# Scans in place of the large reciprocals in the HGRN heads of an encoder block, with ScalarE's side steps pinned behind the weight casts

## The chip, the cores and the metric

The kernel runs on one core of one Trainium2 chip. Its time is device microseconds from start to end, median of 3 runs. TensorE multiplies matrices into PSUM; VectorE (DVE), ScalarE (ACT) and GpSimd (POOL) work on SBUF tiles of 128 partitions; SyncE (SP) issues most transfers. The engines run side by side, each working through its own instructions in a fixed order, and wait for one another by semaphores.

## The reference, cut to what matters

One encoder layer on x of 1024 tokens by 1024 features, all in float32:

```python
h = layer_norm(x, ln_in_g, ln_in_b)
proj = h @ w_in                                # 1024 x 11776
a = dilated_attention(aq, ak, av, slopes)      # 24 heads of 64, three dilations
r = hgrn2(hq, hf_fwd, hf_bwd, hi, hg, ...)     # 8 heads, 128 keys, 128 values
m = sigmoid(ga) * (a @ w_att_up) + sigmoid(gh) * (r @ w_hgrn_up)
h = layer_norm(alpha * h + m @ w_o, ...)
h = layer_norm(alpha * h + (silu(gate) * up) @ w_ffn_out, ...)
```

The change lies in `hgrn2`, in both directions of each head. With the forget gate f = lb + (1 - lb) * sigmoid(f_pre), the recurrence is computed in chunks of the time axis:

```python
cum = jnp.cumsum(log f, axis=time in chunk)
q_dec = q * exp(cum)             # the product of the gates up to a token
k_inv = k * exp(-cum)            # and its reciprocal, k = 1 - f
a = tril(q_dec @ k_inv^T);  o_intra = a @ v
u = (k * exp(cum_last - cum))^T @ v;  S' = exp(cum_last) * S + u
o = o_intra + q_dec @ S
```

So each token needs a running product of gates and the reciprocal of that product.

## The kernel before, in words

**Phase 1** is the input projection as a stream of weights. Its 92 tiles of 128 output columns are done four at a time; each group of four is 14 products (seven products of Strassen's scheme, for two pairs of tiles), and each product is 12 matmuls of 128 x 512, three for each of four blocks of 128 rows, because a float32 weight is split into a high and a low half. For a product, ScalarE casts the high half `w_hi` (L585, function `cast`), VectorE subtracts to get the low half `w_lo` (L590), and TensorE multiplies. `prep(i + 3)` does this three products ahead; four pairs of buffers take turns, so a cast waits until an earlier product has read its pair. Results are evacuated from PSUM by ScalarE (L606) and VectorE (L475, L486, L507).

**Side work.** The loop in `phase1` takes one product per turn and, after it, one part of a side unit. Units are the eight HGRN heads (`hgrn_side`) and, for each of four groups of attention heads, a far and a near part (`att_far`, `att_near`), in the order head, head, far, near. Each unit is a generator: a `yield n` lets n products go by before its next part, and a negative number also allows the next unit's inputs to be fetched. A unit begins when the stream has produced its inputs and the unit before has ended.

**A head's gate stage** is `hgrn_dir`, run for direction 0 and then 1, three parts each, one product apart. Time is laid out in 8 chunks of 128, each of two halves of 64: the "far" half and the "near" half. Part one: ScalarE turns the stored tanh into gates, tile A (the far half, L1262 and L1267) and tile B (the near half and one neighbour, L1263 and L1268), each with a column of zeros that restarts the product; GpSimd turns the tanh tile t in place into 1 - f (L1269); VectorE runs two scans (`tensor_tensor_scan`, L1274) that make running products of A and B in place, with restart constants `self.d1`; GpSimd multiplies the keys' near half by B (L1282). Part two: VectorE takes reciprocals of A, in two instructions of 128 x 256 (L1285), and GpSimd multiplies the keys' far half by them (L1286). Part three: two reciprocals of B (L1289), then the queries are multiplied by A and by the reciprocals (L1290, L1291), and GpSimd copies the chunk ends (L1295, L1296, L1298).

After the gate stage come the transposes of values and keys on TensorE (L905, L1306), copied by ScalarE (L906, L1307), the states (L1322, L1325, L1328, L1336), the scores (L1349 to L1353), the outputs (L1375) and a last transpose (L1411). Slots (`slot(n)`) are ten fixed tiles that the units share; `half` tiles are a ring of five.

**What sets the order.** The program is traced in the order of the Python code, and a planner with its own estimate of durations then puts each engine's instructions in order, by priority and by when it expects their inputs. Casts and evacuations are traced with `high_priority`. The opening and most of the feed-forward part are held in traced order by hand (`in_order`, which adds an order-only edge between neighbours on an engine). The stream and the side work of phase 1 are not: there the planner may put a side instruction ahead of the products that were traced before it.

**Phases 2 and 3** (the merge of attention and HGRN, the output projection, the feed-forward part) follow after about 1207 us and aren't touched.

Of the kernel before, what the change touches and what calls it, by code (L numbers as in the profile page):

```python
# [13 lines left out]
AF = mybir.ActivationFunctionType  # L14
OP = mybir.AluOpType
# [21 lines left out]
CQ = 0.5 * 128 ** -0.5  # L37
# [112 lines left out]
class Block:  # L150
# [405 lines left out]
    def stream(self, tiles):  # L556
# [5 lines left out]
        A = [{}, {}]  # L562
# [31 lines left out]
        def prep(i):  # L594
            if i >= len(seq):
                return
            with tc.high_priority(offset=self.evac_ahead):
                cast(i)
                rest(i, nc.vector)
# [25 lines left out]
        def evacuate(i, *later):  # L625
# [4 lines left out]
            with tc.high_priority(offset=self.evac_ahead):  # L630
# [10 lines left out]
                else:  # L641
                    pair[1](0, ps, None)

        first = 2 * len(self.ORDER)
        with self.pool("p0") as pool:
            self.lasts = {}
# [5 lines left out]
        for i, (n, g, p) in enumerate(seq):  # L652
            if i < first:
                continue
            sums(i + 5)
            prep(i + 3)
            if i < first + 2:
                continue
            product(i)
            evacuate(i)  # L660
            yield 4 * n + 2 * g + 2 if p == 4 else 0
# [588 lines left out]
    def hgrn_dir(self, h, d, st):  # L1250

        nc = self.nc
        ga, gb, gna = (z[:, d, h:h + 1] for z in (self.ga, self.gb, self.gna))
        t3 = st[f"t{d}"].rearrange("p (c i) -> p c i", i=128)
        q3 = st["q"].rearrange("p (c i) -> p c i", i=128)

        A = st["fa"][:, HALF * d:HALF * d + HALF].rearrange("p (c i) -> p c i", i=64)
        B = self.slot(7 + d, "fb", (8, 66))
        if d == 0:
            nc.gpsimd.memset(A[:, :, 0:1], 0.0)  # L1260
            nc.gpsimd.memset(B[:, :, 65:66], 0.0)
            nc.scalar.activation(A[:, :, 1:64], t3[:, :, 65:128], AF.Identity, bias=gb, scale=ga)  # L1262
            nc.scalar.activation(B[:, :, 0:65], t3[:, :, 0:65], AF.Identity, bias=gb, scale=ga)  # L1263
        else:
            nc.gpsimd.memset(A[:, :, 63:64], 0.0)
            nc.gpsimd.memset(B[:, :, 0:1], 0.0)
            nc.scalar.activation(A[:, :, 0:63], t3[:, :, 0:63], AF.Identity, bias=gb, scale=ga)  # L1267
            nc.scalar.activation(B[:, :, 1:66], t3[:, :, 63:128], AF.Identity, bias=gb, scale=ga)  # L1268
        nc.gpsimd.tensor_scalar(t3, t3, gna, ga, op0=OP.mult, op1=OP.add)  # L1269

        def scan(f, n, rev):
            f = f.rearrange("p c i -> p (c i)")
            f = f[:, ::-1] if rev else f
            nc.vector.tensor_tensor_scan(f, f, self.d1[n], 0.0, op0=OP.mult, op1=OP.add)  # L1274

        scan(A, 64, d == 1)
        scan(B, 66, d == 0)
        far = slice(64, 128) if d == 0 else slice(0, 64)
        near = slice(0, 64) if d == 0 else slice(64, 128)
        R = B[:, :, 1:65]  # L1280
        qd = self.slot(2 + 2 * d, "qd", (8, 128))
        nc.gpsimd.tensor_mul(t3[:, :, near], t3[:, :, near], R)  # L1282
        yield
        for c in (slice(0, 4), slice(4, 8)):
            nc.vector.reciprocal(qd[:, c, far], A[:, c])  # L1285
        nc.gpsimd.tensor_mul(t3[:, :, far], t3[:, :, far], qd[:, :, far])  # L1286
        yield
        for c in (slice(0, 4), slice(4, 8)):
            nc.vector.reciprocal(qd[:, c, near], R[:, c])  # L1289
        nc.vector.scalar_tensor_tensor(qd[:, :, far], q3[:, :, far], CQ, A, op0=OP.mult, op1=OP.mult)  # L1290
        nc.vector.scalar_tensor_tensor(qd[:, :, near], q3[:, :, near], CQ, qd[:, :, near], op0=OP.mult, op1=OP.mult)  # L1291
        st["qd", d], st["ki", d] = qd, t3

        dec = st["dec", d] = self.smt.tile([128, 2, 8], F32, name="dec", tag="dec", bufs=4)
        nc.gpsimd.tensor_copy(dec[:, 0, :], A[:, :, 63 if d == 0 else 0])  # L1295
        nc.gpsimd.tensor_copy(dec[:, 1, :], B[:, :, 0 if d == 0 else 65])  # L1296
        both = st["both", d] = self.smt.tile([128, 8], F32, name="both", tag="both", bufs=4)
        nc.gpsimd.tensor_mul(both, dec[:, 0, :], dec[:, 1, :])  # L1298
# [129 lines left out]
    def phase1(self):  # L1428
# [14 lines left out]
        work = self.stream(tiles)  # L1443
        there = next(work)
        self.slp = side.enter_context(self.pool("slp"))
        wait, pre, now, late, free = 0, None, None, -4, True
        for k in work:
            there = k or there
            if now:
                wait -= 1  # L1450
                if wait <= 0:
                    w = next(now, None)
                    if w is None:
                        now = None
                    free = free or w is None or w < 0
                    wait = abs(w or 0)
            if units and there >= units[0][0]:
                n, i, fetch, rest = units[0]
                if free and pre is None:
                    pre = fetch(i)  # L1460
                if now is None:
                    now, wait, free = rest(i, pre), 1, False
                    pre, units = None, units[1:]
            elif not units and not now:
                if late < 0:
                    pass
                elif late == 0:
                    side.close()
                    self.attp, self.stp, resp = (self.pool(z) for z in ("attp", "stp", "resp"))
                    ap, self.sp, self.evp = (z.__enter__() for z in (self.attp, self.stp, resp))  # L1470
                    self.ah, self.al = (ap.tile([128, 4, T], F32R, name=z) for z in ("att_hi", "att_lo"))
                    rs = self.residual(self.sp, self.evp)
                elif late % 3 == 2:
                    next(rs, None)
                elif late % 6 == 4 and late <= 22:
                    i = late // 6
                    self.load_split(self.sp, self.att_d[i], self.ah[:, i, :], self.al[:, i, :],
                                    [slice(0, HALF), slice(HALF, T)])
                late += 1
# [374 lines left out]
    OUT_ROWS = {1: (0, 0), 2: (0, 0), 6: (0, 1), 5: (1, 1), 7: (1, 1), 3: (0, 1)}  # L1854

    @contextmanager
    def in_order(self, free=()):

        traced = self.nc.cur_bb.bb.instructions
        n = len(traced)  # L1860
        yield
        for i in traced[n:]:
            if i.engine in free:
                continue
            before = self.lasts.get(i.engine)
            if before is not None:
                self.tc.add_manual_dep(i, before, mybir.DependencyInfo(mybir.DependencyClass.NoSync,
                                                                       mybir.DependencyReason.DATA), reason="in_order")
            self.lasts[i.engine] = i.name
# [309 lines left out]
```

## Time and profile before

| | |
|---|---|
| time, median of 3 runs | 2091.51 us (2091.43 to 2092.22) |
| the profiled execution | 2092.74 us |
| its span, first to last instruction | 2091.0 us |
| mean granted TensorE clock | 0.994 |
| TensorE busy | 2021.8 us (97%) |
| VectorE busy | 1446.3 us (69%) |
| ScalarE busy | 960.1 us (46%) |
| GpSimd busy | 749.6 us (36%) |

Lines of a profile name an engine, a line of the kernel (L1285), the tiles as out<-in with buffer numbers left out, and shapes as partitions x elements. A group's line ends with its busy time in us, the mean of one instruction in ns, and the engine's idle time just before, with what ended it. A row of waits says who waited for whom: total us, number, longest. A row of busy times by stretch has the stretch, its length, busy us (and number of instructions) of PE (matmul), PEld (weight load), DVE, ACT and POOL, then the granted clock, the share of the DMA engines and GB/s.

### The profile page before, as it was taken

Reading aid. Unit: us, or ns where it says so; the run is one execution under the profiler, and the core shown is the slowest. Engines: PE = TensorE matmul, PEld = TensorE weight load, DVE = VectorE, ACT = ScalarE, POOL = GpSimd, SP = SyncE. Lnnn points to the kernel's source line nnn. Section 1 sums busy time; section 2 is a strip of 40 time slices with the busy share of each in tenths; the row PEclk is TensorE's granted clock in tenths of the full one; section 3 lists DMA queues with packets and bytes.
Section 4 is the critical chain, followed back from the end, with each engine's and each line's share of the span. In section 5 each row is a group of like instructions: output and inputs, shape, how many; then the busy total and the mean of one; then the engine's idle time right before and its main releaser. Section 6 shows DMA issues by size and latency. Waiting matters only on the chain.

```text
span 2091.0 us, 31270 instructions
## 1 busy us (share of the span) xinstructions
PE 2021.8 (97%) x11037; PEld 1673.2 (80%) x11037; DVE 1446.3 (69%) x2361; ACT 960.1 (46%) x2007; POOL 749.6 (36%) x646
## 2 busy tenths in 40 slices
PE   5999999999999999999999999999899999999998
PEld 5778888778888788788888788887688888888876
DVE  7877766886578965877556723447867687777865
ACT  7653555544565536554365431244444444444330
POOL 1212300232013330322200063242667667755553
PEclk9999999999999999999999999999999999999999
DMA  5433533444334352434525774244445445459685
GB/s 206 141 121 126 169 117 110 138 130 141 122 125 140 115 173 97 126 122 136 169 92 176 270 227 131 76 141 136 161 151 170 147 151 182 142 173 321 197 263 168
DMA packets 296447, 324.20 MB, mean 155 GB/s; under 512 B 15905, under 2 KB 212834, under 8 KB 296290
## 3 DMA queue, kind: packets, MB, share of 16 engines
q1 hardware_dynamic: 290272, 302.05, 44.9%
q10 hardware_dynamic: 6018, 20.16, 2.4%
q8 instruction: 87, 1.43, 0.3%
q14 instruction: 70, 0.57, 0.1%
HBM read 211.78 MB, written 110.36 MB: 154 GB/s over the span
## 4 chain that ended last, share of the span: by engine, by line
PE 79%; DVE 8%; issue 4%; DMA 3%; ACT 2%; POOL 2%; DVEq 0%; SPq 0%; ACTq 0%; POOLq 0%
PE pj L301 18%; PE pj L303 18%; PE pj L302 17%; PE sd L303 6%; PE sd L301 6%; PE sd L302 6%; PE sd L1375 2%; DVE w_lo L590 1%; DVE qd L1285 1%; POOL w_lo L280 1%; PE sd L1322 1%; PE sd L1129 1%; PE sd L1184 1%; DVE qd L1289 1%; PE sd L972 1%
## 5 line engine op out<-in xcount | busy, mean ns | idle before, releaser
L585 ACT CAST w_hi<-wa 128x512 fp32r<-128x512 f32 x276 | 169.7, 617 | 236.9 <-PE pj L302 189.1
L590 DVE TENSOR_TENSOR w_lo<-wa,w_hi 128x512 fp32r<-128x512 f32 x273 | 202.1, 743 | 101.6 <-ACT w_hi L585 97.8
L280 POOL TENSOR_TENSOR w_lo<-f_raw,w_hi 128x512 fp32r<-128x512 f32 x110 | 176.0, 1610 | 107.2 <-ACT w_hi L276 45.0
L575 POOL TENSOR_TENSOR wa<-wa,wa 128x512 f32<-128x512 f32 x44 | 62.7, 1425 | 329.0 <-DVE ws L574 196.1
L301 PE MATMUL pj<-xt1hi,w_hi 128*128 128x512 f32 (+1 forms) x276 | 107.4, 389 | 2.4 <-DVE evh L475 2.4
L303 PE MATMUL pj<-xt1hi,w_lo 128*128 128x512 f32 (+1 forms) x276 | 106.7, 387 | 2.0 <-DVE w_lo L590 1.5
L301 PE MATMUL pj<-xb22hi,w_hi 128*128 128x512 f32 x268 | 105.8, 395 | 1.6 <-ACT wkeep L606 1.6
L302 PE MATMUL pj<-xt1lo,w_hi 128*128 128x512 f32 (+1 forms) x276 | 106.7, 387 | 0.0
L303 PE MATMUL pj<-xb22hi,w_lo 128*128 128x512 f32 x268 | 104.9, 393 | 0.5 <-DVE w_lo L590 0.5
L302 PE MATMUL pj<-xb22lo,w_hi 128*128 128x512 f32 x268 | 104.8, 391 | 0.0
L276 ACT CAST w_hi<-f_raw 128x512 fp32r<-128x512 f32 x110 | 67.9, 619 | 79.9 <-DVE f_raw L100 28.6
L280 POOL TENSOR_TENSOR w_lo<-Wb,w_hi 128x512 fp32r<-128x512 f32 x47 | 64.7, 1379 | 58.4 <-ACT w_hi L276 55.7
L301 PE MATMUL pj<-xb11hi,w_hi 128*128 128x512 f32 (+1 forms) x196 | 78.0, 398 | 5.4 <-ACT w_hi L585 2.5
L303 PE MATMUL pj<-xt2hi,w_lo 128*128 128x512 f32 (+1 forms) x196 | 77.3, 396 | 5.5 <-DVE w_lo L590 4.5
L606 ACT COPY wkeep<-pj 128x512 f32<-128x512 f32 x138 | 79.8, 581 | 5.7 <-DVE evh L475 4.1
L301 PE MATMUL pj<-xt2hi,w_hi 128*128 128x512 f32 (+1 forms) x196 | 77.3, 394 | 5.0 <-ACT w_hi L585 3.1
L303 PE MATMUL pj<-xb11hi,w_lo 128*128 128x512 f32 (+1 forms) x196 | 77.2, 394 | 1.5 <-DVE w_lo L590 1.0
L302 PE MATMUL pj<-xt2lo,w_hi 128*128 128x512 f32 (+1 forms) x196 | 76.9, 392 | 0.6 <-DVE xt2lo L432 0.6
L280 POOL TENSOR_TENSOR w_lo<-wsum,w_hi 128x512 fp32r<-128x512 f32 x44 | 66.5, 1510 | 30.5 <-ACT w_hi L276 26.6
L301 PE MATMUL pj<-xt,w_hi 128*128 128x512 f32 x184 | 73.9, 402 | 3.0 <-DVE evh L475 1.7
L301 PE MATMUL pj<-xb21hi,w_hi 128*128 128x512 f32 (+1 forms) x196 | 76.4, 390 | 0.0
L302 PE MATMUL pj<-xb11lo,w_hi 128*128 128x512 f32 (+1 forms) x196 | 76.4, 390 | 0.0
(432 smaller groups left out, 6378.5 us busy)
## 6 DMA issues: line engine op xcount, KB each, us to landing
wa<-in_w_in_dram SPq DMA_DIRECT2D x184, 256.0 KB, 3.1
f_raw<-in_w_ffn_in_dram SPq DMA_DIRECT2D x44, 512.0 KB, 4.2
Wb<-in_w_ffn_out_dram SPq DMA_DIRECT2D x40, 256.0 KB, 5.3
tg<-evh SPq DMA_DIRECT2D x32, 256.0 KB, 2.3
tg<-tg SPq DMA_DIRECT2D x16, 512.0 KB, 4.2
y<-ahs SPq DMA_DIRECT2D x16, 512.0 KB, 3.6
ah<-xt SPq DMA_DIRECT2D x8, 512.0 KB, 6.3
rec<-hg ACTq DMA_DIRECT2D x8, 512.0 KB, 4.2
```

The lines of the kernel that those rows point to most:

```text
L276: nc.scalar.copy(hi, src)
L280: e.tensor_sub(lo, src, hi.bitcast(F32))
L301: nc.tensor.matmul(ps, whi, xhi, start=first, stop=False, **kw)
L302: nc.tensor.matmul(ps, whi, xlo, start=False, stop=False, **kw)
L303: nc.tensor.matmul(ps, wlo, xhi, start=False, stop=last, **kw)
L575: third.tensor_sub(a["a21"], a["a11"], a["a21"])
L585: nc.scalar.copy(ready[i][0], A[g][self.PRODUCTS[p][0]])
L590: e.tensor_sub(lo, A[g][self.PRODUCTS[p][0]], hi.bitcast(F32))
L606: nc.scalar.copy(t, ps)
L972: nc.tensor.matmul(ps[:, 192 * h:192 * h + 192], q[HD[hd], 256 * r + 128 * h:256 * r + 128 * h + 128], k[HD[hd], 256 * r + 64 * h:256 * r ...
L1129: nc.tensor.matmul(ps[:, tt % 2, :], q[pb, 128 * tt - 64:128 * tt + 64], k[pb, 128 * (tt - 1):128 * (tt + 1)], start=True, stop=True)
L1375: nc.tensor.matmul(po[:, jj, :], l, r, start=(n == 0), stop=(n == len(terms) - 1))
```

## The change

Three things are changed in phase 1.

The four large reciprocals of a direction go. Instead, ScalarE computes the gates twice more, into G (laid over half of the query tile `qd`) and H (a `half` tile), shifted by one token against A and B. VectorE takes the reciprocal of the eight chunk ends only, writes them into the first column of each chunk of `ends` (a `half` tile that GpSimd has set to zero), and a scan in the opposite direction multiplies the gates onto them: the reciprocal of a running product is the reciprocal of the whole product times the gates that are still to come. L1269, which writes t in place, comes after all four gate activations that read t.

ScalarE's instructions of a side part get an order-only edge to the last ScalarE instruction of `sums` and `prep` traced in the same turn, which is the cast for the product three ahead (`noted` and `behind`).

A unit that is fetched and begun in the same turn waits for two products instead of one.

```diff
+        self.ahead_of = {}
...
-            sums(i + 5)
-            prep(i + 3)
+            with self.noted():
+                sums(i + 5)
+                prep(i + 3)
...
         B = self.slot(7 + d, "fb", (8, 66))
...
+        qd = self.slot(2 + 2 * d, "qd", (8, 128))
+        G = qd[:, 0:4, :].rearrange("p a (b i) -> p (a b) i", i=64)
+        H = self.half("finv").rearrange("p (c i) -> p c i", i=64)
+        ends = self.half("ends").rearrange("p (c i) -> p c i", i=64)
+        R = B[:, :, 1:65]
+
+        def gates(f, one, to, of):
+            nc.gpsimd.memset(f[:, :, one:one + 1], 0.0)
+            nc.scalar.activation(f[:, :, to], t3[:, :, of], AF.Identity, bias=gb, scale=ga)
+
+        lo, hi = slice(0, 63), slice(1, 64)
+        nc.gpsimd.memset(ends, 0.0)
+        if fwd:
+            gates(A, 0, hi, slice(65, 128))
+            gates(B, 65, slice(0, 65), slice(0, 65))
+            gates(G, 63, lo, slice(65, 128))
+            gates(H, 0, hi, slice(1, 64))
...
         nc.gpsimd.tensor_scalar(t3, t3, gna, ga, op0=OP.mult, op1=OP.add)
...
+        def inverse(f, of, rev):
+            nc.vector.reciprocal(ends[:, :, 0], of[:, ::-1] if rev else of)
+            scan(f, ends.rearrange("p c i -> p (c i)"), rev)
...
-        for c in (slice(0, 4), slice(4, 8)):
-            nc.vector.reciprocal(qd[:, c, far], A[:, c])
-        nc.gpsimd.tensor_mul(t3[:, :, far], t3[:, :, far], qd[:, :, far])
+        inverse(G, A[:, :, 63 if fwd else 0], fwd)
+        nc.gpsimd.tensor_mul(t3[:, :, far], t3[:, :, far], G)
         yield
-        for c in (slice(0, 4), slice(4, 8)):
-            nc.vector.reciprocal(qd[:, c, near], R[:, c])
+        inverse(H, R[:, :, 0 if fwd else 63], not fwd)
         nc.vector.scalar_tensor_tensor(qd[:, :, far], q3[:, :, far], CQ, A, op0=OP.mult, op1=OP.mult)
-        nc.vector.scalar_tensor_tensor(qd[:, :, near], q3[:, :, near], CQ, qd[:, :, near], op0=OP.mult, op1=OP.mult)
+        nc.vector.scalar_tensor_tensor(qd[:, :, near], q3[:, :, near], CQ, H, op0=OP.mult, op1=OP.mult)
...
-                    w = next(now, None)
+                    with self.behind((E.Activation,)):
+                        w = next(now, None)
...
-                if free and pre is None:
+                new = free and pre is None
+                if new:
                     pre = fetch(i)
                 if now is None:
-                    now, wait, free = rest(i, pre), 1, False
+                    now, wait, free = rest(i, pre), 2 if new else 1, False
...
+    def noted(self):
+        traced = self.nc.cur_bb.bb.instructions
+        n = len(traced)
+        yield
+        for i in traced[n:]:
+            self.ahead_of[i.engine] = i.name
...
+    def behind(self, engines):
+        traced = self.nc.cur_bb.bb.instructions
+        n = len(traced)
+        yield
+        for i in traced[n:]:
+            if i.engine in engines and i.engine in self.ahead_of:
+                self.tc.add_manual_dep(i, self.ahead_of[i.engine], ...NoSync..., reason="behind")
```

More of the change, by code (lines that the diff above doesn't have):

```diff
@@ L1255, in hgrn_dir @@
         q3 = st["q"].rearrange("p (c i) -> p c i", i=128)
+        fwd = d == 0
+        far = slice(64, 128) if fwd else slice(0, 64)
+        near = slice(0, 64) if fwd else slice(64, 128)
         A = st["fa"][:, HALF * d:HALF * d + HALF].rearrange("p (c i) -> p c i", i=64)
         B = self.slot(7 + d, "fb", (8, 66))
[L1259 to L1263, printed above, removed]
-        else:
[L1265 to L1268, printed above, removed]
+        qd = self.slot(2 + 2 * d, "qd", (8, 128))
@@ L1269, in hgrn_dir, with scan @@
+        if fwd:
[3 more added lines that the diff above has]
+            gates(H, 0, hi, slice(1, 64))
+        else:
+            gates(A, 63, lo, slice(0, 63))
+            gates(B, 0, slice(1, 66), slice(63, 128))
+            gates(G, 0, hi, slice(0, 63))
+            gates(H, 63, lo, slice(64, 127))
         nc.gpsimd.tensor_scalar(t3, t3, gna, ga, op0=OP.mult, op1=OP.add)
-        def scan(f, n, rev):
+        def scan(f, at, rev):
@@ L1272, in scan @@
             f = f.rearrange("p c i -> p (c i)")
             f = f[:, ::-1] if rev else f
[L1274 to L1281, printed above, removed]
+            nc.vector.tensor_tensor_scan(f, f, at, 0.0, op0=OP.mult, op1=OP.add)
@@ L1282, in hgrn_dir @@
+        def inverse(f, of, rev):
+            nc.vector.reciprocal(ends[:, :, 0], of[:, ::-1] if rev else of)
+            scan(f, ends.rearrange("p c i -> p (c i)"), rev)
+        scan(A, self.d1[64], not fwd)
+        scan(B, self.d1[66], fwd)
         nc.gpsimd.tensor_mul(t3[:, :, near], t3[:, :, near], R)
         yield
[L1284 to L1286 removed]
+        inverse(G, A[:, :, 63 if fwd else 0], fwd)
@@ L1856, in in_order @@
     @contextmanager
+    def noted(self):
[4 more added lines that the diff above has]
+            self.ahead_of[i.engine] = i.name
+    @contextmanager
+    def behind(self, engines):
[4 more added lines that the diff above has]
+            if i.engine in engines and i.engine in self.ahead_of:
+                self.tc.add_manual_dep(i, self.ahead_of[i.engine],
+                                       mybir.DependencyInfo(mybir.DependencyClass.NoSync,
+                                                            mybir.DependencyReason.DATA), reason="behind")
+    @contextmanager
     def in_order(self, free=()):
```

1 line of the change is left out of this document (added).

## The prediction

> **What bounds the kernel now.** I read the page's head first, then the table of waits of TensorE for the stretch 90 to 1160 us (the weight stream of the input projection, in which all eight HGRN heads and four attention groups run as side work), then busy times by stretch, and last the instructions of VectorE, GpSimd and ScalarE around single waits.
>
> ```profile
> span 2091.0 us, 31270 instructions
> PE 2021.8 (97%) x11037; PEld 1673.2 (80%) x11037; DVE 1446.3 (69%) x2361; ACT 960.1 (46%) x2007; POOL 749.6 (36%) x646
> ```
>
> TensorE is busy 97% of the span and the change takes no matmul away, so the only thing to be won is TensorE's idle time. In the stretch where the changed lines run, its waits are these (who waited, for whom: us in total, times, longest):
>
> ```profile
> PE pj L303 <- DVE w_lo L590: 7.5, 8, 2.9
> PE sd L1306 <- POOL t L1282: 4.3, 2, 2.7
> PE pj L301 <- DVE evh L475: 4.2, 3, 1.7
> PE sd L1306 <- POOL t L1286: 2.4, 2, 1.8
> PE pj L301 <- DVE wkeep L507: 1.9, 1, 1.9
> PE sd L1411 <- DVE hon L1382: 0.9, 1, 0.9
> ```
>
> That is 21.2 us in two classes. VectorE's own results (the low halves of weights at L590, evacuations at L475 and L507, the normalised output at L1382) come late for 7.5 + 4.2 + 1.9 + 0.9 = 14.5 us in 13 waits. The keys that the key transposes (L1306) need come late from GpSimd for 4.3 + 2.4 = 6.7 us in 4 waits. No wait here names ScalarE, and none names an attention step. To see that they sit in the heads' gate stage, I asked for busy times in eight stretches, one for each head's gates; the last two and the sum over all eight are (length, then busy of TensorE, weight loads, VectorE, ScalarE, GpSimd, then granted clock):
>
> ```profile
> 868.00:890.00 22.00, 18.54 (x82) 14.84 (x81) 20.85 (x21) 9.30 (x17) 11.94 (x12) 0.92 0.30 106
> 928.00:968.00 40.00, 36.79 (x182) 30.01 (x181) 35.35 (x36) 16.94 (x33) 15.08 (x21) 1.00 0.30 99
> sum 232.00, PE 210.60 PEld 171.99 DVE 218.36 ACT 102.86 POOL 96.38; mean PE 26.32 PEld 21.50 DVE 27.29 ACT 12.86 POOL 12.05
> ```
>
> In these 232 us TensorE idles 232.0 - 210.6 = 21.4 us, which is all of its waits, and VectorE is busy 218.4 us or 94%. ScalarE is at 44% and GpSimd at 42%. So VectorE is the scarce engine exactly where TensorE waits. Behind three of the waits the granted clock, the number after the busy times, is low (0.55, 0.69, 0.56):
>
> ```profile
> 381.80:384.90 3.10, 3.10 (x10) 2.55 (x11) 3.10 (x4) 0.59 (x1) 1.99 (x5) 0.55 0.29 83
> 439.50:445.00 5.50, 4.93 (x15) 3.66 (x16) 5.50 (x6) 1.53 (x3) 0.62 (x1) 0.69 0.26 96
> 880.00:883.90 3.90, 3.88 (x10) 3.04 (x11) 3.90 (x3) 0.00 (x0) 1.09 (x1) 0.56 0.24 67
> ```
>
> The clock costs 0.45 x 3.1 + 0.31 x 5.5 + 0.44 x 3.9 = 1.4 + 1.7 + 1.7 = 4.8 us more; the first belongs to the key class (it follows the 2.7 us wait of L1306), the other two to VectorE's. So VectorE's class is worth 14.5 + 3.4 = 17.9 us, the keys' class 6.7 + 1.4 = 8.1 us, and 26.0 us is the most that this change can win, give or take what modelled matmul ends hide.
>
> **The change part by part: reciprocals.** What an item of VectorE, ScalarE and GpSimd costs, by shape:
>
> ```profile
> L1285 DVE RECIPROCAL qd<-fa 128x256 f32<-128x256 f32 x32 | 53.8, 1713 | 0.0
> L1289 DVE RECIPROCAL qd<-fb 128x256 f32<-128x256 f32 x32 | 53.8, 1713 | 0.0
> ...
> L1225 DVE RECIPROCAL lbm<-lbm 128x16 f32<-128x16 f32 x1 | 0.2, 240 | 0.0
> ```
>
> Removed are all 64 large reciprocals: 53.8 + 53.8 = 107.6 us. Added are 32 reciprocals over 8 columns and 32 scans over 512. The trace has no reciprocal of 8 columns; it lies between nothing and the 0.24 us of 16 columns, and I take 0.24, the nearest row: 7.7 us. The scan's two ends are in its own record, next to the key product at L1282 on GpSimd (ns, least/median/most):
>
> ```profile
> L1274 DVE TENSOR_TENSOR_SCAN fb<-fb,d x16: 1185/1255/2096, 97.1 to 961.0; 128x528 f32<-128x528 f32 x16
> L1282 POOL TENSOR_TENSOR t<-t,fb x16: 1172/1194/2182, 100.2 to 963.7; 128x512 f32<-128x512 f32 x16
> ```
>
> At the median 32 scans are 40 us, at the most 67. So VectorE is relieved by 107.6 - 7.7 - 40 = 60 us, or 33 at the worst end. In the eight stretches its load falls from 94% to about 68%, or 80%. What that does to the path is read at a wait, the one of 2.9 us at 880:
>
> ```profile
> 875.32 3.33 DVE L1285 RECIPROCAL qd<-fa 128x256 f32<-128x256 f32 x2
> 878.58 1.38 DVE L590 TENSOR_TENSOR w_lo<-wa,w_hi 128x512 fp32r<-128x512 f32 x1
> 879.88 1.74 DVE L1289 RECIPROCAL qd<-fb 128x256 f32<-128x256 f32 x1
> ```
>
> The weights' low half stands right behind a pair of reciprocals and had TensorE waiting as it began. A small reciprocal and a scan take 0.24 + 1.25 = 1.5 us in the pair's place, so what stands behind one pair comes 1.8 us earlier, behind two pairs 3.7. All 13 waits of the class are 2.9 us or shorter, most near 1, so one or two pairs ahead suffice. I keep 15% for what a changed order leaves: 0.85 x 17.9 = 15.2 us won.
>
> The Trainium skill has a rule against this: its GPSIMD Engine Reference, section "Key points", says that GpSimd shares its SBUF interfaces with VectorE and contends with VectorE instructions that have two SBUF inputs. A scan reads two, a reciprocal one; the spread of both rows above agrees with it. Rival B, below, is worked out from these rows alone.
>
> **ScalarE and GpSimd.** Each direction of a head gets two more gate activations and three more memsets:
>
> ```profile
> L1263 ACT ACTIVATE fb<-t,gb,ga 128x520 f32<-128x520 f32 x8 | 6.6, 824 | 5.8 <-PE sd L1375 5.8
> ...
> L1262 ACT ACTIVATE fa<-t,gb,ga 128x504 f32<-128x504 f32 x8 | 6.4, 800 | 13.6 <-DMA t<-hg4t 5.2 <-DMA t<-hg2t 5.1 <-DMA t<-hg6t 3.3
> ```
>
> ```profile
> L1261 POOL MEMSET fb<- 128x8 f32 x8 | 0.9, 114 | 16.4 <-DMA att<-ol 12.7 <-issue 3.7
> ...
> L1239 POOL MEMSET d<- 128x512 f32 x1 | 0.5, 525 | 0.0
> ```
>
> ScalarE: 32 x 0.80 = 25.6 us; GpSimd: 32 x 0.11 + 16 x 0.53 = 12 us. Neither lies on the path by its sum: in the eight stretches ScalarE goes from 103 to at most 129 us of 232, GpSimd from 96 to 108. What does lie on a chain is that the in-place key factor (L1269, GpSimd) now waits for four gates instead of two, 1.6 us later in each direction; if ScalarE's cover were gone, that would be 16 x 1.6 = 26 us. The two extra half-row buffers per direction come from a ring of five whose earlier tenants (the previous head's squares and outputs) are read before the head ends; I cost them at nothing, with GpSimd's queue as the cover and one 0.53 us memset per direction, 8 us, as the price without it.
>
> **The pin.** ScalarE's instructions of a side step now stand behind the cast that the stream issued three products ahead in that step. In the record they run far ahead of it, as at head 5:
>
> ```profile
> 678.42 0.79 ACT L1267 ACTIVATE fa<-t,gb,ga 128x504 f32<-128x504 f32 x1
> ...
> 682.67 0.62 ACT L585 CAST w_hi<-wa 128x512 fp32r<-128x512 f32 x1 [1.67 <-PE pj L302]
> 683.20 0.58 ACT L606 COPY wkeep<-pj 128x512 f32<-128x512 f32 x1
> 685.83 0.62 ACT L585 CAST w_hi<-wa 128x512 fp32r<-128x512 f32 x1 [2.05 <-PE pj L302]
> 688.55 0.62 ACT L585 CAST w_hi<-wa 128x512 fp32r<-128x512 f32 x1 [2.10 <-PE pj L302]
> 691.90 0.62 ACT L585 CAST w_hi<-wa 128x512 fp32r<-128x512 f32 x1 [2.72 <-PE pj L302]
> ```
>
> Counting the loop's steps, head 5's first part is pinned behind the cast at 682.67 and its second direction (L1267) behind that at 691.90: this gate moves back by 13 us, the first direction's by about 5. A step is 2.7 us (two casts, 685.83 and 688.55). ScalarE's own stores of a head's or an attention part's result are pinned in the same way; they wait for VectorE anyway. Queued behind a gate are the next casts, which are ready three products, 8 us, ahead of use and wait about 2 us each for a buffer anyway; that is the cover. From gates to key transposes the code leaves six steps, 16 us, in the first direction and five, 13.6, in the second; four gates (3.2), two scans (2.5), L1282 (1.2), the small reciprocal with its scan (1.5) and the far key product (1.3, as at 378.89 below) need 9.7, so the slack is 6.6 and 3.9 us. The gain of the pin is on the other side: gates no longer crowd VectorE while the previous head ends. I book it at nothing, with bounds of +2 us per head lost (16) and the keys' class (8) won.
>
> **One step later.** By the loop's counts a unit is fetched and begun in the same step only at heads 0 and 3 and the far attention parts 2 and 3. Heads 2, 4 and 6, whose gates show waits for a transfer in the L1262 row above, are fetched a step before they begin and don't count as fresh, so those waits stay. What moves with the step are the fetches that the unit's parts issue on SP's queue (the values in the first part, the output gate in the sixth), each past two weight loads at most. The side work ends one step, 2.7 us, later, far ahead of the projection's end; I take 0.
>
> **The keys' class** is a chain on GpSimd, here before the wait that ends at 381.75 (chain of waits: start, us):
>
> ```profile
> 373.51 3.94 POOL t L1269 x2
> ...
> 378.89 1.23 POOL t L1286
> 380.12 1.59 POOL t L1282
> ```
>
> No reciprocal is in it. The pin takes the second direction's L1269 out from before the first one's products (2 us better), the two gates put 1.6 back. I let a third of the class go: 2.7 us. **Sum:** 15.2 + 2.7 = 17.9, rounded 18. The profiled execution took 2092.7 us (span 2091.0 and 1.7 around it), 1.2 above the median; 2092.7 - 18 - 1.2 = 2073.5, called 2073.
>
> **The clock.** The Trainium skill, TensorE: Matmul & The Clock Gate, section "What's actually happening", drops the clock to half after an idle window of about 3.4 us. Here waits of 2.7 and 2.9 us were enough for 0.55. By the Trainium skill's figure no wait here should have cost clock, and the sum would be a gain of 15 instead of 18; I go by the rows.
>
> **The rivals.** A, the forecast: 2066 to 2081, 57%. B, contention: every scan beside GpSimd costs its most, and L1282 and L1286 with it; half of VectorE's class stays (9 us won), the keys' class wins nothing: 2091.5 - 9 = 2082.5. For it: 2.10 and 2.18 us above, against 1.19 for L1282 beside reciprocals. Against it: medians sit at the low end. 18%. C, no change: the waits are of order, not load, and re-form behind whatever stands there (scans of 2 us, evacuations): gain 1, 2090.5. For it: L590 waits though its lead is 8 us. Against it: two reciprocals in a row directly ahead. 13%. D, slower: the pinned gates are late at the key transposes L1306. A direction loses a step (2.7) and two gates (1.6) and saves one pair (1.8): 2.5 us over its slack in all 16 is 40 us, less A's 15 from VectorE's class: 2116; it decides from 15 / 16, about 1 us per direction. For it: four waits of L1306 already. Against it: slacks of 6.6 and 3.9 us. 12%.
>
> **Numbers.** The time is A's, 2073. 2063 to 2091 takes in the 26 us bound with 2.5 more for modelled ends, B and half of C, and leaves out D. What a measurement of this kernel tells from no change is about 0.2%, 4.2 us: A and B are faster, 75%; C is within, 13%; D is slower, 12%.
>
> **What would show it.** After: waits for L590, L475 and L507 under 3 us in total, VectorE about 60 us less busy, ScalarE 26 more; scans at a median near 1.25. If scans sit near 2, it is B; waits for L590 still at 7, C; waits for L1306 above 15 us, D. That heads 2, 4, 6 no longer wait for their transfer would show my reading of the third edit wrong.

## The result, and the profile after

The changed kernel takes 2073.24 us (median of 4 runs, 2071.14 to 2074.03), the kernel before 2091.47 in the same comparison: a ratio of 0.9912, 95% interval 0.99 to 0.9923. The forecast was 2073. The total is right; the experiments will show that it was right for a wrong reason.

The head of the page of the kernel after:

```profile
span 2071.7 us, 31393 instructions
PE 2013.5 (97%) x11037; PEld 1672.6 (81%) x11037; DVE 1407.2 (68%) x2361; ACT 975.6 (47%) x2039; POOL 792.0 (38%) x694
```

VectorE has 39 us less to do (1446.3 before), where 60 were forecast; ScalarE has 16 more (26 forecast) and GpSimd 42 more (12 forecast).

TensorE's waits of the kernel after, for the same stretch 90 to 1160 us:

```profile
PE pj L303 <- DVE w_lo L590: 6.8, 3, 3.4
PE sd L1368 <- DVE hR L1352: 1.4, 1, 1.4
PE sd L1193 <- DVE p L932: 1.1, 1, 1.1
PE pj L301 <- DVE evh L475: 0.9, 1, 0.9
PE sd L1186 <- DVE p L932: 0.5, 1, 0.5
```

That is 10.7 us against 21.6 before (the prediction's 21.2 and two rows of 0.2). The keys' class (the key transposes, now L1322, waiting for GpSimd) has no row left: all 6.7 us are gone, not a third. VectorE's class, which should have nearly vanished, is all that is left, 10.7 us against 14.5; 6.8 of them are at L590, in fewer and longer waits: 3 instead of 8. Two of these three make up nearly all of the 6.8, and behind both the clock falls, as these stretches of the kernel after show (the columns are those of the prediction's stretches):

```profile
383.10:387.10 4.00, 3.97 (x10) 3.12 (x11) 4.00 (x6) 1.05 (x4) 1.68 (x2) 0.57 0.16 59
632.20:636.20 4.00, 3.96 (x10) 3.13 (x11) 4.00 (x6) 1.66 (x3) 0.00 (x0) 0.57 0.66 209
```

The clock still costs 0.43 x 4 x 2 = 3.4 us, against 4.8 before. So waits and clock account for 10.9 + 1.4 = 12 of the 19.3 us by which the span is shorter. The rest is in no row of the table of waits. The heads of the two pages show where it lies: TensorE's busy time fell by 2021.8 - 2013.5 = 8.3 us for the same 11037 matmuls, of which the clock is 1.4, and its idle time by only 11.0. Since the ends of matmuls are modelled, I can't place the rest better. But it is won in the weight stream. One row times that stream: the group of L590's subtractions with its first and last start, here in the kernel before, the kernel after, and one experiment (the changed kernel with the key factor on ScalarE, below):

```profile
L590 DVE TENSOR_TENSOR w_lo<-wa,w_hi x273: 618/685/1783, 29.5 to 1197.3; 128x512 fp32r<-128x512 f32 x137
```

```profile
L590 DVE TENSOR_TENSOR w_lo<-wa,w_hi x273: 620/686/1797, 28.4 to 1177.8; 128x512 fp32r<-128x512 f32 x137
```

```profile
L590 DVE TENSOR_TENSOR w_lo<-wa,w_hi x273: 624/685/1778, 29.4 to 1169.1; 128x512 fp32r<-128x512 f32 x137
```

From first to last start it runs 1167.8 us before, 1149.4 after (18.4 less, the whole gain), and 1139.7 in the experiment.

The scans and the small reciprocals on VectorE, kernel after (ns, least/median/most); the scans over `fa` and `fb` were there before, those over `qd` (G) and `finv` (H) are new.

```profile
L1291 DVE TENSOR_TENSOR_SCAN fa<-fa,d x16: 1205/1218/2218, 121.1 to 932.2; 128x512 f32<-128x512 f32 x16
L1291 DVE TENSOR_TENSOR_SCAN fb<-fb,d x16: 1220/1240/2285, 122.8 to 933.3; 128x528 f32<-128x528 f32 x16
L1291 DVE TENSOR_TENSOR_SCAN qd<-qd,ends x16: 1210/1224/2216, 124.6 to 935.5; 128x512 f32<-128x512 f32 x16
L1291 DVE TENSOR_TENSOR_SCAN finv<-finv,ends x16: 1209/1795/2222, 126.6 to 937.7; 128x512 f32<-128x512 f32 x16
L1295 DVE RECIPROCAL ends<-fa x16: 168/184/206, 124.0 to 934.5; 128x8 f32<-128x8 f32 x16
L1295 DVE RECIPROCAL ends<-fb x16: 192/195/207, 126.4 to 937.4; 128x8 f32<-128x8 f32 x16
```

A small reciprocal takes 0.19 us where I took 0.24. Three of the scans have the forecast median, 1.22 to 1.24 us (1.25 was forecast); the last, over H, has 1.80. The other part of the shortfall is in the weights' low halves, before and then after (groups of VectorE in the stretch 90 to 1160 us: busy us, mean ns):

```profile
L590 DVE TENSOR_TENSOR w_lo<-wa,w_hi 128x512 fp32r<-128x512 f32 x247 | 183.0, 743 | 97.0 <-ACT w_hi L585 93.3 <-PE sd L972 2.0 <-DMA at2q<-evh 1.3
```

```profile
L590 DVE TENSOR_TENSOR w_lo<-wa,w_hi 128x512 fp32r<-128x512 f32 x252 | 198.9, 792 | 96.8 <-ACT w_hi L585 94.3 <-PE sd L974 2.0 <-PE sd L1028 0.3
```

At 49 ns more each, 252 of them cost VectorE 12 us.

### The profile page after: what moved, and what is told of

Same layout as the page of the kernel before. It is cut to its first block, busy times and chain, and to the rows that moved or that the text cites. A ratio compares the mean times of both kernels' runs of the same rounds, so it can differ in the third digit from the quotient of the medians.

```text
span 2071.7 us, 31393 instructions
## 1 busy us (share of the span) xinstructions
PE 2013.5 (97%) x11037; PEld 1672.6 (81%) x11037; DVE 1407.2 (68%) x2361; ACT 975.6 (47%) x2039; POOL 792.0 (38%) x694
## 4 chain that ended last, share of the span: by engine, by line
PE 77%; DVE 8%; DMA 5%; issue 4%; ACT 3%; POOL 2%; DVEq 0%; SPq 0%; ACTq 0%; POOLq 0%
PE pj L301 17%; PE pj L303 17%; PE pj L302 16%; PE sd L301 6%; PE sd L303 6%; PE sd L302 6%; PE sd L1391 2%; DVE w_lo L590 2%; DMA wa<-in_w_in_dram 2%; PE sd L1338 1%; POOL w_lo L280 1%; DMA ghi<-gs3h 1%; PE sd L1206 1%; ACT pf L1011 1%; PE sd L1131 1%
## 5 line engine op out<-in xcount | busy, mean ns | idle before, releaser
L590 DVE TENSOR_TENSOR w_lo<-wa,w_hi 128x512 fp32r<-128x512 f32 x273 | 213.8, 787 | 100.3 <-ACT w_hi L585 97.7
L575 POOL TENSOR_TENSOR wa<-wa,wa 128x512 f32<-128x512 f32 x44 | 67.3, 1531 | 245.0 <-DVE ws L574 156.3
L303 PE MATMUL pj<-xb21hi,w_lo 128*128 128x512 f32 (+1 forms) x196 | 75.9, 387 | 3.4 <-DVE w_lo L590 3.4
L301 PE MATMUL pj<-xt3hi,w_hi 128*128 128x512 f32 x188 | 75.2, 400 | 1.5 <-ACT w_hi L276 1.5
```

What stands on the lines that cost most here:

```text
L301: nc.tensor.matmul(ps, whi, xhi, start=first, stop=False, **kw)
L303: nc.tensor.matmul(ps, wlo, xhi, start=False, stop=last, **kw)
L575: third.tensor_sub(a["a21"], a["a11"], a["a21"])
L590: e.tensor_sub(lo, A[g][self.PRODUCTS[p][0]], hi.bitcast(F32))
```

## The experiments

Each kernel below is the kernel before or after with the edit shown, timed against the kernel before on the same chip (medians of the latter 2091.0 to 2091.8). In their rows the line numbers shift with the edits: the key transposes are L1306 before, L1308 to L1323 elsewhere; the weights' low half is L590 in all.

| kernel | median us | ratio to before, 95% |
|---|---|---|
| after (scans, all of ScalarE's side steps pinned, later start) | 2073.2 | 0.9912 (0.99 to 0.9923) |
| scans alone | 2089.6 | 0.9992 (0.9982 to 1.0002) |
| pin alone | 2074.3 | 0.9918 (0.9901 to 0.9934) |
| later start alone | 2093.0 | 1.0009 (0.9999 to 1.0018) |
| scans and pin | 2081.1 | 0.995 (0.9934 to 0.9965) |
| pin and later start | 2076.9 | 0.9935 (0.9918 to 0.9952) |
| pin of the gates alone | 2074.4 | 0.992 (0.9904 to 0.9936) |
| pin of all but the gates | 2096.9 | 1.0028 (1.0017 to 1.0039) |
| copies for the reciprocals | 2084.7 | 0.9964 (0.9952 to 0.9976) |
| gates pinned, key factor on ScalarE | 2069.4 | 0.9904 (0.9887 to 0.992) |
| after, key factor on ScalarE | 2064.5 | 0.9868 (0.9854 to 0.9882) |
| scans, gates pinned | 2078.4 | 0.9942 (0.9929 to 0.9956) |
| gates pinned, copies for the reciprocals | 2075.3 | 0.9929 (0.9914 to 0.9945) |

The first question is which of the three edits carries the gain. The prediction had put all but 2.7 us of it on the scans.

### The scans alone

```diff
 the changed kernel without the pin and the later start
-                    with self.behind((E.Activation,)):
-                        w = next(now, None)
+                    w = next(now, None)
...
-                    now, wait, free = rest(i, pre), 2 if new else 1, False
+                    now, wait, free = rest(i, pre), 1, False
```

> The scans alone, without the pin and without the later start. Theory 1 (VectorE's load carries the gain): about 2076 us, 15 us won, TensorE's waits for w_lo, evh and wkeep under 5 us, and the waits of L1322 (key transposes) for GpSimd still some 5 us. Theory 2 (the order of ScalarE's gates carries it, since gates drawn ahead let both directions and the previous head's end crowd VectorE): about 2087 us, w_lo still 5 us or more. Theory 3 (the later start): 2080 or more.

Measured: 2089.64 us, a ratio whose interval reaches 1. VectorE is relieved as in the changed kernel (1410.4 us busy), and TensorE's waits are these:

```profile
PE pj L303 <- DVE w_lo L590: 8.8, 6, 4.6
PE sd L1322 <- POOL t L1303: 5.9, 2, 4.1
```

L590 still has 8.8 us (7.5 before), the key transposes 5.9 (6.7 before). This is rival C of the prediction, waits that re-form, and it holds for the scans by themselves.

### The pin alone

```diff
 the kernel before, with its reciprocals
+                    with self.behind((E.Activation,)):
+                        w = next(now, None)
-                    w = next(now, None)
```

> The pin alone, with the large reciprocals kept. Theory 1: 2090 us, no change, or slower, since VectorE keeps its 107.6 us of reciprocals. Theory 2: about 2079 us, with the waits for GpSimd's keys gone and w_lo below 4 us.

Measured: 2074.31 us, within 1.1 us of the whole change, with all 64 large reciprocals still there (VectorE 1447.0 us busy, as before). Waits of L590 are 2.2 us, those of the key transposes 0.9:

```profile
PE pj L303 <- DVE w_lo L590: 2.2, 3, 0.9
...
PE sd L1308 <- POOL t L1288: 0.9, 2, 0.5
```

So the part that I booked at nothing is worth about 17 us, twice the 8 us that I gave as the most it could win.

### The later start alone

```diff
 the kernel before
-                    now, wait, free = rest(i, pre), 1, False
+                    now, wait, free = rest(i, pre), 2 if new else 1, False
```

> The later start alone, which by the loop's counts delays only heads 0 and 3 and the far parts 2 and 3 by a step. Theories 1 and 2: within 4 us of 2091.5. Theory 3: 2085 or less.

Measured: 2093.02 us, no change that can be told. The waits of the gates for their transfer, which a later start might have been thought to shorten, are there (17.5 us at this line against 13.6 before):

```profile
L1264 ACT ACTIVATE fa<-t,gb,ga 128x504 f32<-128x504 f32 x8 | 6.4, 800 | 17.5 <-DMA t<-hg4t 7.0 <-DMA t<-hg6t 5.6 <-DMA t<-hg2t 4.9
```

### Scans and pin, pin and later start

```diff
 the changed kernel without the later start
-                    now, wait, free = rest(i, pre), 2 if new else 1, False
+                    now, wait, free = rest(i, pre), 1, False
```

> Scans and pin, without the later start. Theories 1 and 2: 2073 to 2075 us, as with all three. Theory 3: 2080 or more, with waits for a head's transfer back on ScalarE.

```diff
 the kernel before with the pin and the later start, reciprocals kept
+                    with self.behind((E.Activation,)):
+                        w = next(now, None)
-                    w = next(now, None)
...
-                    now, wait, free = rest(i, pre), 1, False
+                    now, wait, free = rest(i, pre), 2 if new else 1, False
```

> Pin and later start, with the large reciprocals: the change without its scans. The earlier runs have scans alone at 2090, pin alone at 2074, both at 2081, all three at 2073. Theory 2 (the pin carries the gain, the scans nothing): 2072 to 2077 us. If the scans are needed beside the pin and the later start: 2085 or more.

Measured: 2081.07 and 2076.86 us. On top of the pin (2074.3) the scans cost 6.8 us and the later start 2.6, of which the first has intervals that only touch (0.9934 in both) and the second has intervals that overlap; all three together give 2073.2. So the later start takes 7.8 us off a kernel with scans and pin, though it wins nothing elsewhere. I have no row that explains that interaction. The idle time of the pinned gates shows what the later start does to the transfers, with the pin alone and with both:

```profile
L1264 ACT ACTIVATE fa<-t,gb,ga 128x504 f32<-128x504 f32 x8 | 6.5, 806 | 5.4 <-DMA t<-hg4t 5.4
```

```profile
L1264 ACT ACTIVATE fa<-t,gb,ga 128x504 f32<-128x504 f32 x8 | 6.5, 806 | 0.0
```

The pin takes the transfer waits of heads 2 and 6 away, because it holds the gates back until the data is there; the later start takes head 4's.

### Which part of the pin: the gates, or all the rest

`behind` reaches every ScalarE instruction of a side part. Two kernels split it, both with the reciprocals and no later start: in the first only the four gate activations of a head are ordered behind the cast, in the second everything but them.

```diff
 gates alone
+            with self.behind((mybir.EngineType.Activation,)):
-            nc.scalar.activation(A[...], t3[...], AF.Identity, bias=gb, scale=ga)
-            nc.scalar.activation(B[...], t3[...], AF.Identity, bias=gb, scale=ga)
+                nc.scalar.activation(A[...], t3[...], AF.Identity, bias=gb, scale=ga)
+                nc.scalar.activation(B[...], t3[...], AF.Identity, bias=gb, scale=ga)
```

> Only the gate activations of the heads are pinned, with the large reciprocals; no other side instruction is. Theory 2a (the pin works because gates no longer run ahead and both directions and the previous head's end no longer crowd VectorE): the whole gain, about 2075 us. Theory 2b (it works through the other side instructions of ScalarE, attention, copies and states, that stood ahead of casts): 2088 or more.

```diff
 all but the gates: the gates are marked and left out of behind()
-            if i.engine in engines and i.engine in self.ahead_of:
+            if i.engine in engines and i.engine in self.ahead_of and i.name not in self.free:
```

> Every side instruction of ScalarE but the gates is pinned, with the large reciprocals. Theory 2a: about 2091 us, no gain. Theory 2b: about 2075 us.

Measured: 2074.40 us with the gates alone, 2096.85 without them. So the gates' order is the whole of the pin's gain, and the order of the rest is no help by itself (5 us slower).

What the order changes is best seen at head 6, where the kernel before has its 2.9 us wait. ScalarE's gates there, kernel before (L1262 and L1263 are the first direction, L1267 and L1268 the second):

```profile
863.27 0.81 ACT L1262 ACTIVATE fa<-t,gb,ga 128x504 f32<-128x504 f32 x1 [3.27 <-DMA t<-hg6t]
...
870.70 0.81 ACT L1267 ACTIVATE fa<-t,gb,ga 128x504 f32<-128x504 f32 x1 [2.55 <-DMA t<-hg6t]
871.42 0.81 ACT L1268 ACTIVATE fb<-t,gb,ga 128x520 f32<-128x520 f32 x1
...
873.13 0.83 ACT L1263 ACTIVATE fb<-t,gb,ga 128x520 f32<-128x520 f32 x1
```

and the two key factors (L1269) on GpSimd that follow them, the second direction's first:

```profile
872.34 1.95 POOL L1269 TENSOR_SCALAR t<-t,gna,ga 128x1024 f32<-128x1024 f32 x1 [0.19 <-ACT fb L1268]
...
876.87 1.20 POOL L1269 TENSOR_SCALAR t<-t,gna,ga 128x1024 f32<-128x1024 f32 x1
```

The planner has put both of the second direction's gates ahead of the first's tile B (L1263); only the first's tile A was earlier. That it did so because that tile B has yet to wait for an attention transfer (`att<-ol`, which reads the same slot) is read from the code and from GpSimd's memset of it (L1261), which waits 6.4 us for that transfer and runs at 872.03; the planner's own reason is not shown. So both directions' scans, reciprocals and products pile up at once, and the first direction's keys, which TensorE needs first, come last: the reciprocals around the late low half in the prediction's rows (875.32 and 879.88) are the second direction's, and the first's scan of B starts only at 883.16. Heads 2 and 4 have the same crossing in the kernel before. With the gates ordered (L1265, L1266 and then L1271, L1272), the same head:

```profile
853.28 0.81 ACT L1265 ACTIVATE fa<-t,gb,ga 128x504 f32<-128x504 f32 x1
...
860.60 0.83 ACT L1266 ACTIVATE fb<-t,gb,ga 128x520 f32<-128x520 f32 x1 [3.97 <-DMA att<-ol]
...
862.85 0.81 ACT L1271 ACTIVATE fa<-t,gb,ga 128x504 f32<-128x504 f32 x1
863.56 0.82 ACT L1272 ACTIVATE fb<-t,gb,ga 128x520 f32<-128x520 f32 x1
```

The first direction comes first, though ScalarE now idles 4 us for the transfer. The crossing is a part of the account, not all of it: the waits of TensorE in these three heads' stages are 8.3 of the 21.6 us. In heads 1, 3, 5 and 7 of the kernel before, the second direction's tile A comes right behind the first's gates, 27 to 29 us ahead of its own tile B, and how that makes TensorE wait is not followed here. Nor does a run order the two directions without also holding both behind a cast, so the crossing and the early start are not told apart. The row that overturns the prediction is the sum over eight stretches of 29 us, each starting at a head's first gate, in the kernel with the gates ordered:

```profile
sum 232.00, PE 226.62 PEld 188.66 DVE 227.68 ACT 112.19 POOL 105.59; mean PE 28.33 PEld 23.58 DVE 28.46 ACT 14.02 POOL 13.20
```

VectorE is busy 227.7 of 232 us, 98%, and TensorE idles 5.4 us. The prediction's stretches were laid around the waits; cut by the rule used here, 29 us from each head's first gate, the kernel before has VectorE busy 217.3 us, again 94%, and TensorE idle 19.0. So a VectorE that is even fuller makes TensorE wait far less: its load by itself was not what made TensorE wait.

### Copies in place of the reciprocals

The scans might have failed only because they are dear themselves. So in the kernel before the 64 reciprocals were replaced by copies of the same shape; the reciprocals are thereby left out of the computation.

```diff
-            nc.vector.reciprocal(qd[:, c, far], A[:, c])
+            nc.vector.tensor_copy(qd[:, c, far], A[:, c])
...
-            nc.vector.reciprocal(qd[:, c, near], R[:, c])
+            nc.vector.tensor_copy(qd[:, c, near], R[:, c])
```

> The kernel before with each large reciprocal replaced by a copy of the same shape, so the reciprocals are left out and what follows computes with the products themselves. No scan, no gate, no pin is added; VectorE is relieved by some 85 to 95 us. Theory 1 in its purest form: 2073 to 2077 us. Theory 2: at least half of the 26 us of waits stay or re-form elsewhere, 2083 or more.

And the same with the gates ordered, which leaves out the reciprocals as well:

> The heads' gate activations ordered behind the casts, and the 64 large reciprocals replaced by copies of the same shape (so the reciprocals are left out of the computation). It bounds what any cheaper way to the reciprocals can win once the gates are in order. Without that order the copies won 6.8 us. If VectorE's load no longer sets TensorE's waits then: 2071 to 2075, within 3 us of the 2074.4 with reciprocals. If load still counts (the prediction's view of 0.85 of VectorE's waits): 2068 us or less.

Measured: 2084.74 us without the order, 6.8 us won. The copies are not free: one takes 0.28 us at the median over A and 1.10 over B, so VectorE is relieved by 52 us (1446.3 to 1394.4 busy) where the expectation had 85 to 95. That is about the relief that the change was to bring, not the whole price of the reciprocals. L590 keeps its waits:

```profile
PE pj L303 <- DVE w_lo L590: 9.7, 6, 4.3
```

One of them is 2.7 us long and ends at 877.75. The low half that it is for starts at 877.01, behind two copies, a scan and a query product that keep VectorE busy from 871.89 on, 5.1 us in a row.

With the gates ordered it is 2075.34 us against 2074.40 with the reciprocals, with intervals that overlap: 54 us less on VectorE (1445.3 to 1391.0) win nothing that can be told. So VectorE's load has no visible price left there, some without the order (6.8 us for 52), and the forecast's step from 60 us of relief to 15 us of time falls.

### The scans with the gates ordered

```diff
 the gates' order, and the change's G, H, ends and inverse()
         def gates(f, one, to, of):
             nc.gpsimd.memset(f[:, :, one:one + 1], 0.0)
-            nc.scalar.activation(f[:, :, to], t3[:, :, of], AF.Identity, bias=gb, scale=ga)
+            with self.behind((mybir.EngineType.Activation,)):
+                nc.scalar.activation(f[:, :, to], t3[:, :, of], AF.Identity, bias=gb, scale=ga)
```

> Scans in place of the large reciprocals, only the heads' gate activations ordered behind the casts, no later start. Beside it stand the gates' order with the reciprocals kept (2074.4), the scans alone (2089.6), and scans with all of ScalarE's side instructions ordered (2081.1). If the gates' order is the cause of the gain and the scans win nothing on top: 2072 to 2077. If relief of VectorE adds to it, 2066 to 2071. If the scans take something back, as in the run with all side instructions ordered: 2079 to 2083.

Measured: 2078.42 us, between two of the expectations' bands; beside 2074.40 the scans win nothing, and whether they cost the 4 us can't be told from intervals that overlap slightly (0.9929 to 0.9956, 0.9904 to 0.9936). It agrees in sign with the 6.8 us above.

### The key factor on ScalarE

What is left of TensorE's waits in the changed kernel are two at L590. This is VectorE ahead of the first, in time order (start, us):

```profile
375.88 2.29 DVE L1291 TENSOR_TENSOR_SCAN fb<-fb,d 128x528 f32<-128x528 f32 x1
378.09 0.66 DVE L1306 SCALAR_TENSOR_TENSOR qd<-q,fa 128x512 f32<-128x512 f32 x1
378.67 0.68 DVE L1307 SCALAR_TENSOR_TENSOR qd<-q,finv 128x512 f32<-128x512 f32 x1
379.27 0.19 DVE L1295 RECIPROCAL ends<-fa 128x8 f32<-128x8 f32 x1
379.39 1.50 DVE L576 TENSOR_TENSOR wa<-ws,wa 128x512 f32<-128x512 f32 x1
380.81 0.68 DVE L513 SCALAR_TENSOR_TENSOR evh<-evh,wkeep 128x512 f32<-128x512 f32 x1
381.41 1.67 DVE L590 TENSOR_TENSOR w_lo<-wa,w_hi 128x512 fp32r<-128x512 f32 x1
```

and busy times of the stretch that ends with that wait: GpSimd, the fifth, is as full as VectorE, the third.

```profile
374.00:383.10 9.10, 5.74 (x34) 4.59 (x32) 9.10 (x10) 5.58 (x12) 9.10 (x8) 1.00 0.17 61
```

The scan, the sum and the low half take 2.29, 1.50 and 1.67 us, against medians of 1.24 for that scan and 0.69 for the low half. So one of the two largest pieces of GpSimd's work there, the key factor (2.20 us from 378.15 on), was moved to ScalarE, once with the reciprocals and the gates ordered, once in the changed kernel.

```diff
-        nc.gpsimd.tensor_scalar(t3, t3, gna, ga, op0=OP.mult, op1=OP.add)
+        nc.scalar.activation(t3, t3, AF.Identity, bias=ga, scale=gna)
```

> The kernel before, with its reciprocals, the heads' gate activations alone ordered behind the casts (2074.4 us as measured), and the key factor (L1269, which turns t in place into 1 - f, 2.3 us on GpSimd) moved to ScalarE as one activation of 128x1024. Theory K: what is left of TensorE's waits in the gate stages comes from GpSimd's key factor running beside VectorE's instructions and from the chain through it; then this takes 2066 to 2071 us. Theory N: the key factor lies beside other work once the gates are ordered; then 2073 to 2076. Rival R: the activation, some 1.3 us on ScalarE ahead of the casts, delays the casts; then above 2078.

> The changed kernel (2073.2 us) with the key factor moved to ScalarE. Its scans read two inputs and were 1.28 to 1.68 us in the mean beside GpSimd, 1.2 at the least. Theory K: the key factor beside the scans is what keeps them slow; then scan means fall to 1.25 to 1.35 us, the waits on the weights' low half (6.8 us) to under 3, and the time to 2064 to 2070 us. Theory N: 2072 to 2075. Rival R (ScalarE's casts late): above 2077.

Measured: 2069.40 us with the reciprocals (its interval meets that of the gates' order alone, so a gain of 5 is likely and not certain), and 2064.47 us in the changed kernel, 8.8 us faster than it, with intervals that don't meet. That is the fastest kernel of this study. Its waits for L590, and VectorE at the same place:

```profile
PE pj L303 <- DVE w_lo L590: 1.0, 2, 0.6
```

```profile
379.31 1.25 DVE L1291 TENSOR_TENSOR_SCAN fb<-fb,d 128x528 f32<-128x528 f32 x1
380.48 0.66 DVE L576 TENSOR_TENSOR wa<-ws,wa 128x512 f32<-128x512 f32 x1
...
381.74 0.69 DVE L590 TENSOR_TENSOR w_lo<-wa,w_hi 128x512 fp32r<-128x512 f32 x1
```

The three instructions are back at 1.25, 0.66 and 0.69 us, 2.9 us less, and no wait for L590 is over 0.6 where one was 3.4; TensorE's longest wait in the stretch is now 2.0 us, for ScalarE's copy of transposed keys (L1323). The expectation on the scans was wrong all the same: those over H stay slow, with a median of 1.91 us:

```profile
L1291 DVE TENSOR_TENSOR_SCAN finv<-finv,ends x16: 1209/1908/2316, 127.3 to 932.1; 128x512 f32<-128x512 f32 x16
```

So the move frees the places where TensorE waited, and the scans over H are no faster. That less sharing is the cause at that place, and not the shorter chain on GpSimd or a shifted order, is argued from these durations; no run separates them. In the changed kernel the key factor ran beside the slow sum (L576), but the slow scan ran beside GpSimd's other large piece, the weights' sum L575 (374.85 to 377.06).

## Why the prediction was right in its total and wrong in its reasons

**What bounds the kernel.** That the gain lies in the stream held: it is 18.4 us shorter, which is all of it. That it is all idle time held less well: idle time fell by 11.0 us, and 8.3 came out of what the profile counts as busy, where the prediction had only the clock and "modelled matmul ends". The statement that no wait names ScalarE or an attention step left out two rows of 0.2 us (L1322 for ScalarE's L1307, L1034 for L930), which changes nothing. "So VectorE is the scarce engine exactly where TensorE waits" was the first false step. VectorE was full where TensorE waited (94%), but it is fuller (98%) where TensorE hardly does, once the gates are ordered. A share of busy time next to a wait was taken for its cause.

**The reciprocals, 15.2 us.** This is the term that failed: 0.85 of 17.9 us. Alone the scans give 2.2 us, by an interval that reaches 1, and copies, with 52 us of relief, 6.8. The error is in "one or two pairs ahead suffice": it assumed that the instructions behind a removed pair keep their places. With another order to choose, the planner puts other side work there, as in the 5.1 us above; L590 waits 8.8 us with scans and 9.7 with copies. Rival C named just that ("the waits are of order, not load") at 13%, and was right about the scans; its sign, "waits for L590 still at 7", came with 6.8 in the kernel after.

**VectorE's relief, 60 us.** It was 39. The scans of the kernel after, by their groups (busy us, mean ns):

```profile
L1291 DVE TENSOR_TENSOR_SCAN finv<-finv,ends 128x512 f32<-128x512 f32 x16 | 26.9, 1680 | 0.5
...
L1291 DVE TENSOR_TENSOR_SCAN qd<-qd,ends 128x512 f32<-128x512 f32 x16 | 22.4, 1403 | 0.6 <-POOL dec L1311 0.2
```

The two new ones take 49.3 us instead of 40, the small reciprocals 32 x 0.19 = 6.1 instead of 7.7; so the relief is 107.6 - 55.4 = 52 us, and the low halves give 12 of it back. Rival B's mechanism is real and was priced at the wrong place, as the last section shows.

**ScalarE and GpSimd.** That neither engine came to bound the time held. ScalarE's instructions did get 25 us longer in all (the new gates' own durations are 25.5, as forecast); its busy time grew by 16 because it counts once what overlapping records share, and gates that follow one another overlap: they start 0.71 us apart and last 0.81 (862.85 and 863.56 above). GpSimd's 42 us more was far off: 11 us of it are the memsets, near the 12 worked out there; the rest, which the forecast put at nothing, is slower instructions: the two key products 15 us, the copies of chunk ends and their product (L1311, L1312, L1314) 16, with the key factor 6 us faster. The last section shows the product with B.

**The pin, 0 us.** The second term that failed, and the larger. I saw that gates "no longer crowd VectorE while the previous head ends" and that the second direction's key factor leaves the first one's products alone, and booked them at nothing and at "2 us better". They are worth 17 us. The rows of the pin alone place 11 of it: 5.3 at L590 (7.5 to 2.2) and 5.8 at the keys (6.7 to 0.9); the clock behind such waits and time that no row names are the rest. The bounds were wrong because the gain was capped at the keys' class, 8 us: I hadn't allowed that the order of gates decides VectorE's waits. The cover that I named did hold: no wait of the kernel after in this stretch names a cast. Rival D (gates late at the key transposes) fell with it, since no such wait is left.

**The later start, 0 us.** Alone it is nothing, as forecast. That heads 2, 4 and 6 "are fetched a step before they begin", so that "those waits stay", was wrong as announced: no gate of the kernel after waits for its head's transfer. The pin removes two of the three waits and the later start the third. In the kernel with scans and pin the later start is worth 7.8 us, which stays unexplained.

**The keys' class, 2.7 us.** A third was to go; all went, 6.7 us and the clock behind it, nearly all by the pin: with the pin alone 0.9 us stay, with the scans alone 5.9.

**The clock.** Two waits of 3.4 and 2.9 us left the clock at 0.57 for about 4 us. The Trainium skill, TensorE: Matmul & The Clock Gate, section "What's actually happening", puts the idle window at about 3.4 us. The second wait is below it; as in the kernel before, the rows decide for the shorter wait.

So 18 us came out by luck, because two errors of 13 and 14 us cancelled: the scans were given 15.2 and won 2.2 alone, the pin with the keys' class was given 2.7 and won 17. The scans were credited with the gain that the gates' order has.

## What to carry to other kernels

An engine that is nearly full where another waits need not be the cause; look first at which instruction stands ahead of the late one, and whether it had to be there. Where a planner orders side work freely, work that becomes ready early can be drawn ahead of what is needed soon, and an order-only edge on the first link of that work can be worth more (17 us here) than taking 52 us of it away (6.8). Before crediting a change of several edits to its largest one, time the edits apart.

## What the runs showed of the hardware that was not expected

Scans on VectorE slow GpSimd's products by more than most of the scans are slowed themselves. GpSimd's product of the keys and B took 1.19 us at the median in the kernel before (L1282). Here it is in the kernel after, then with the scans alone, and then with the gates ordered and the reciprocals kept (ns, least/median/most):

```profile
L1300 POOL TENSOR_TENSOR t<-t,fb x16: 1200/1702/2106, 127.4 to 936.4; 128x512 f32<-128x512 f32 x16
```

```profile
L1300 POOL TENSOR_TENSOR t<-t,fb x16: 1195/1682/2181, 101.5 to 956.6; 128x512 f32<-128x512 f32 x16
```

```profile
L1286 POOL TENSOR_TENSOR t<-t,fb x16: 1193/1202/1640, 123.8 to 936.9; 128x512 f32<-128x512 f32 x16
```

With the scans it is 1.70 and 1.68 us whatever the order, and without them 1.20 with the new order: half a microsecond for a product of 128 x 512. But a scan is not the only instruction that does it: with copies for the reciprocals and the old order, where no scan is added, the median is 1.63. Taken one by one with what VectorE ran meanwhile, the 16 products of the kernel before show why: the twelve that ran beside reciprocals alone took 1.17 to 1.21 us, the three that ran partly or wholly beside the weights' subtractions, such as L590, which read two tiles, 1.57 to 1.64, and the one partly beside a scan 2.18. In the kernel after, twelve ran at least partly beside a scan and took 1.64 to 2.11. The Trainium skill, GPSIMD Engine Reference, section "Key points", names contention with VectorE instructions that have two SBUF inputs. A scan and a low half have two, a reciprocal hasn't; these rows agree with it.
